# PSUM banks chosen by the scheduler, a reordered first load and warm-up matmuls in an eight-core decoder kernel

## Chip, cores and metric

The kernel runs on all 8 cores of one Trainium2 chip. The metric is the device time of the slowest core, in microseconds (us). The program has a second, slower state: in some executions the cores of one die get a lower clock, and the time is some per cent longer (in one slow run of experiment 9, cores 4 to 7 had a mean granted clock of 0.807 to 0.810 and the time was 1508.9 us, where the fast runs took 1339.9 and 1341.6 us). The granted clock is the share of TensorE's full clock that the chip granted, as the profile records it.

## The reference, cut to what matters

Two layers of a hybrid decoder. Each layer normalises its input, projects it into q, k, v, gates and a rank-16 "alpha_low", runs gated linear attention and a causal pooling mixer, and merges the two branches.

```python
xn = rmsnorm(h, norm_g)
q, k, v, ga, u, gb, alow, mg = jnp.split(xn @ w_in, IN_OFFSETS, axis=-1)
la = jax.nn.log_sigmoid(alow @ w_alpha + b_alpha) / GATE_TAU     # alow has 16 columns
...                                                              # linear attention with forget gate la
y_pool = pool_mix(u, 0, 0, pool_w, pool_scale)                   # trailing means over 2, 4, 8, 16
ya = (rms(o) * gla_gain * silu(ga)) @ w_a
yb = (y_pool * silu(gb)) @ w_b
return h + (s_a * ya + s_b * yb) @ w_out, S_new, buf_new
```

Each core takes one prompt of 2048 tokens and 16 samples of 4 tokens. The prompt is worked on in 16 token tiles of 128, two to a pair: pairs p0 to p7. The sample tokens and the 16 meta tokens form one more block of 80 columns, called p8. Phase 1 of a layer goes through p0 to p7 and then p8; phase 2 merges the branches.

## The kernel before

The program is recorded as a list of operations and then list-scheduled: each engine takes, among its operations that are ready, the one that stands first in the program. The program gives out 8 PSUM banks. Before, this is done in program order while the list is recorded, least recently freed first; the scheduler moves operations afterwards, but cannot change a bank.

```python
class Banks:
    def pair(self):                       # two neighbouring banks, freed longest ago
        c = [s for s in range(0, 8, 2) if s in self.freed and s + 1 in self.freed]
        s = min(c, key=lambda s: (max(self.freed[s], self.freed[s + 1]), s))
        del self.freed[s], self.freed[s + 1]
        return (s, s + 1)
    # ... one(), free()

def decay(l, p):
    n = ntok(p)                           # 256, or 80 for p8
    xn = xn_of(p)
    b1 = banks.one()
    for kc in range(8):                   # "alow": 16 weight columns
        mm(bank(b1)[0:16, 0:n], V1[:, kc * 16:kc * 16 + 16], xn[:, kc, 0:n], kc == 0, kc == 7)
    cp("act", alow[0:16, 0:n], bank(b1)[0:16, 0:n])      # one buffer "alow" for all pairs
    banks.free(b1)
    b2 = banks.pair()
    for h in range(4):                    # "alpha": 17 rows, fp32
        mm(bank(b2)[:, h * n:(h + 1) * n], walpha[0:17, h * 128:(h + 1) * 128], alow[0:17, 0:n], True, True)
    # ... exp, ln, scan, exp on ScalarE and VectorE

def v_proj(p, i):
    b_ = banks.pair()
    # ... 16 matmuls of 128x512, then one copy on ScalarE
    banks.free(b_)

def phase1(l):
    front(l, 0); front(l, 1)
    if l == 0:
        pace(len(queue), False)           # all weight loads
    decay(l, 0); decay(l, 1)
    # ... v of four tiles, then q, k of two pairs
    for p in range(NPAIR):
        if p >= 2:
            decay(l, p); v_proj(p, 0); v_proj(p, 1); q_proj(p); k_proj(p)
        # ... k_tok, gate_a, scores, attend, pool_u, attend
        gate_b(l, p)
        # ... normalise, gate_o, front(l, p + 2)
        pool_y(l, p)                      # needs the window sums of GpSimd
        # ... gate_o
    decay(l, NPAIR)                       # the block p8
    # ... the rest of p8
```

Of the kernel before, what the change touches and what calls it, by code (L numbers as in the profile page):

```python
# [49 lines left out]

class Sched:
# [4 lines left out]
    def __init__(self):  # L56
        self.ops = []
        self.last_w = {}
        self.readers = {}
        self.cache = {}  # L60

    def grains(self, x):
        if isinstance(x, (str, tuple)):
            return (x,)
        t = x.tensor.name
        esz = 4 if x.dtype == F32 else 2
        dims = [(int(s), int(n)) for s, n in x.ap]
        key = (t, esz, int(x.offset), tuple(dims))
        g = self.cache.get(key)
        if g is None:  # L70
            row = dims[0][0]
            lo = int(x.offset) % row
            hi = lo + sum(s * (n - 1) for s, n in dims[1:]) + 1
            if t == "psum":
                g = tuple(("B", b) for b in range(lo * esz // 2048, (hi * esz - 1) // 2048 + 1))
            else:
                g = tuple(range(lo * esz // GR, (hi * esz - 1) // GR + 1))
            self.cache[key] = g
        return g

    def add(self, eng, fn, r=(), w=(), dma=False, after=(), cost=300.0, lat=100.0, attach=False):
        i = len(self.ops)
        deps = {}
        rg = [g for x in r for g in self.grains(x)]
        wg = [g for x in w for g in self.grains(x)]
        excl = set(g for g in rg if isinstance(g, tuple) and g[0] == "B")
        for g in rg:
            d = self.last_w.get(g)
            if d is not None:
                deps[d] = "RAW"  # L90
        for g in excl:
            for e, d in self.readers.get(g, ()):
                if e != eng and d not in deps:
                    deps[d] = "WAR"
        for g in wg:
            d = self.last_w.get(g)
            if d is not None and d not in deps:
                deps[d] = "WAW"
            for _, d in self.readers.get(g, ()):
                if d not in deps:  # L100
                    deps[d] = "WAR"
        for d in after:
            if d is not None:
                deps[d] = "RAW"
        for g in rg:
            self.readers.setdefault(g, []).append((eng, i))
        for g in wg:
            self.last_w[g] = i
            self.readers[g] = []
        deps.pop(i, None)  # L110
        self.ops.append(dict(eng=eng, fn=fn, deps=deps, dma=dma, token=None, cost=float(cost), lat=float(lat),
                             attach=attach))
        return i
# [7 lines left out]
    def list_schedule(self):  # L121
        ops = self.ops
# [14 lines left out]
        for i in range(n):  # L137
            if npred[i] == 0:
                heapq.heappush(pend[ops[i]["eng"]], (0.0, i))
        order = []  # L140
        start_t = {}
        while len(order) < n:
            best = None
            for e in engs:
                T = free_t[e]
                while pend[e] and pend[e][0][0] <= T:
                    heapq.heappush(avail[e], heapq.heappop(pend[e])[1])
                if avail[e]:
                    st_, idx = T, avail[e][0]
                elif pend[e]:  # L150
                    st_, idx = pend[e][0]
                else:
                    continue
                if best is None or (st_, idx) < (best[0], best[1]):
                    best = (st_, idx, e)
            st_, idx, e = best
            if avail[e] and avail[e][0] == idx:
                heapq.heappop(avail[e])
            else:
                heapq.heappop(pend[e])  # L160
# [6 lines left out]
            else:  # L167
                free_t[e] = st_ + op["cost"]
                done_t[idx] = st_ + op["cost"] + op["lat"]
            order.append(idx)  # L170
# [156 lines left out]
class Banks:  # L327


    def __init__(self):  # L330
        self.freed = {b: b - 8 for b in range(8)}
        self.clock = 0

    def pair(self):
        c = [s for s in range(0, 8, 2) if s in self.freed and s + 1 in self.freed]
        assert c, "no pair of banks"
        s = min(c, key=lambda s: (max(self.freed[s], self.freed[s + 1]), s))
        del self.freed[s], self.freed[s + 1]
        return (s, s + 1)

    def one(self):
        lone = [b for b in self.freed if (b ^ 1) not in self.freed]
        c = lone or list(self.freed)
        assert c, "no bank"
        b = min(c, key=lambda b: (self.freed[b], b))
        del self.freed[b]
        return (b,)

    def free(self, bs):
        for b in bs:  # L350
            assert b not in self.freed
            self.clock += 1
            self.freed[b] = self.clock


def build_nc():
# [34 lines left out]
    with contextlib.ExitStack() as st:  # L391
# [3 lines left out]
        banks = Banks()  # L395
# [78 lines left out]
        vtok.append(bf(v2_off + 8192, 1024))  # L474

# [25 lines left out]
        def mm(out, lhsT, rhs, start, stop, sgc=False):  # L501
# [3 lines left out]
            return S.add("pe", lambda e: e.matmul(out, lhsT=lhsT, rhs=rhs, start=start, stop=stop,  # L505
# [3 lines left out]
        def tr(out, in_, ident):  # L509
            c = 58.0 if in_.dtype != F32 else 220.0  # L510
            return S.add("pe", lambda e: e.transpose(out, in_, ident), r=[in_, ident], w=[out], cost=c, lat=250.0,  # L511
                         attach=True)

        def act(out, in_, func, bias=None, scale=None, accum_out=None):
# [17 lines left out]
            return S.add("act", lambda e: e.activation(out=out, in_=in_, func=func, **kw), r=r, w=w, cost=c)  # L532
# [8 lines left out]
        def tt(eng, out, in0, in1, op):  # L541
# [3 lines left out]
            return S.add(eng, lambda e: e.tensor_tensor(out=out, in0=in0, in1=in1, op=op), r=[in0, in1], w=[out], cost=c)  # L545

        def ts(eng, out, in0, s1, s2=None, op0=ALU.mult, op1=None):
# [4 lines left out]
            return S.add(eng, lambda e: e.tensor_scalar(out=out, in0=in0, **kw), r=r, w=[out],  # L552
                         cost=ecost(eng, fsz(out), 0.55, [out] + r))

        def stt(out, in0, scalar, in1, op0, op1):
            r = [in0, in1] + ([] if isinstance(scalar, float) else [scalar])
            return S.add("dve", lambda e: e.scalar_tensor_tensor(out=out, in0=in0, scalar=scalar, in1=in1, op0=op0,  # L557
# [3 lines left out]
        def cp(eng, out, in_):  # L561
            if eng == "act":
                return act(out, in_, AF.Copy)
            return S.add(eng, lambda e: e.tensor_copy(out=out, in_=in_), r=[in_], w=[out],  # L564
# [15 lines left out]
        def bank(bs):  # L580
            return psum[:, bs[0] * 512:bs[0] * 512 + 512 * len(bs)]

        def bbank(bs):
            return psum[:, bs[0] * 512:bs[0] * 512 + 512].bitcast(BF16)
# [5 lines left out]
        cft = f32(base, NCF)  # L590
        dma(cft, cf_d[:, :])
        dma(cols, cols_d[:, :])
        for t in range(2):
            dma(hb[t], hin[128 * t:128 * (t + 1), :])
# [15 lines left out]
        W1V = [(0, O_V)] + [(O_V + 2048 * i, O_V + 2048 * (i + 1)) for i in range(8)]  # L610
# [41 lines left out]
        def norm_t(l, h, n, k, dst):  # L652
# [3 lines left out]
            b_ = banks.one()  # L656
# [5 lines left out]
            banks.free(b_)  # L662

        def front(l, p):

            if l == 0:
                for i, t in enumerate(tiles_of(p)):
                    r0, n = rows(t)
                    h = hb[t % 2][0:n, :]
                    if t >= 2:  # L670
                        dma(h, hin[r0:r0 + n, :], eng="pool" if t < 4 else "sp")
# [17 lines left out]
        def decay(l, p):  # L689
# [3 lines left out]
            b1 = banks.one()  # L693
# [3 lines left out]
            banks.free(b1)  # L697
            b2 = banks.pair()
# [4 lines left out]
            banks.free(b2)  # L703
# [25 lines left out]
        def q_proj(p):  # L729
# [3 lines left out]
            b_ = banks.pair()  # L733
# [3 lines left out]
            banks.free(b_)  # L737

        def k_proj(p):
# [3 lines left out]
            b_ = banks.pair()  # L743
# [3 lines left out]
            banks.free(b_)  # L747
# [4 lines left out]
        def v_proj(p, i):  # L752
# [4 lines left out]
            b_ = banks.pair()  # L757
            for b in range(2):
                for kc in range(8):
                    mm(bank(b_)[0:n, b * 512:(b + 1) * 512], xn[:, kc, i * 128:i * 128 + n],  # L760
                       WV[:, kc * 1024 + b * 512:kc * 1024 + (b + 1) * 512], kc == 0, kc == 7)
            cp("act", v_[0:n, :], bank(b_)[0:n, :])
            banks.free(b_)

        def k_tok(p, k_):

            n = ntok(p)
            b_ = banks.one()
# [17 lines left out]
            banks.free(b_)  # L786

        def scores(p, i, q_, k_):
            N = ntok(p)
            n = 128 if p < NPAIR else NM  # L790
            b_ = banks.one()
# [6 lines left out]
            banks.free(b_)  # L798
# [9 lines left out]
        def attend(p, i, q_, v_):  # L808

            t = tiles_of(p)[i]  # L810
            bo = banks.pair()
# [6 lines left out]
            bp = banks.pair()  # L818
# [9 lines left out]
            banks.free(bp)  # L828
            return bo

        def normalise(bo, n, dst, k):
# [12 lines left out]
            banks.free(bo)  # L844

        def gate_o(src, n, egv, dst):
            b_ = banks.one()
# [4 lines left out]
            banks.free(b_)  # L852

        def gate_a(l, p, r):
# [4 lines left out]
            b_ = banks.pair()  # L859
# [4 lines left out]
            banks.free(b_)  # L864
# [14 lines left out]
        def pool_u(l, p):  # L879
            n = ntok(p)  # L880
            xn = xn_of(p)
            b_ = banks.pair()
# [7 lines left out]
            if p < NPAIR:  # L890
                cp("act", ue[:, :, 15:271], u3)
                banks.free(b_)
# [13 lines left out]
            banks.free(b_)  # L906
# [10 lines left out]
        def pool_state(l):  # L917
# [3 lines left out]
            for rt in range(2):  # L921
                sp_ = xb[rt].bitcast(F32)[0:120, :]
                dma(sp_, spool[l].rearrange("s p c -> (s p) c")[rt * 120:(rt + 1) * 120, :])
                b_ = banks.one()
# [4 lines left out]
                banks.free(b_)  # L929

        def pool_out(l):
# [5 lines left out]
            b_ = banks.one()  # L937
# [4 lines left out]
            banks.free(b_)  # L942
            for k in range(TS):
                dma(nsp_s[l, :, 11 + k, :], tmpB[k * NSS:(k + 1) * NSS, 0:512])
            b_ = banks.one()
# [3 lines left out]
            banks.free(b_)  # L949
            dma(nsp_p[l], tmpB[0:15, 512:1024])  # L950

        def gate_b(l, p):
            n = ntok(p)
            xn = xn_of(p)
            b_ = banks.pair()
# [5 lines left out]
            banks.free(b_)  # L961

        def pool_y(l, p):
            n = ntok(p)
            b_ = banks.pair()
# [8 lines left out]
            banks.free(b_)  # L974
# [3 lines left out]
        def phase1(l):  # L978
            memset("dve", alow[0:17, :], 1.0)
            dma(walpha[0:17, :], walpha_d[l])  # L980
            front(l, 0)
            front(l, 1)
            if l == 0:
                pace(len(queue), False)
            decay(l, 0)
            decay(l, 1)
# [4 lines left out]
            for f_ in (q_proj, k_proj):  # L991
                for p in range(2):
                    f_(p)
                    if l > 0:
                        pace()
# [52 lines left out]
            bp = banks.pair()  # L1048
# [7 lines left out]
            banks.free(bp)  # L1056
# [17 lines left out]
        def sample_write(l, s, hp):  # L1074
            b_ = banks.one()
# [7 lines left out]
            banks.free(b_)  # L1083
# [3 lines left out]
        def sample_o(l, bT):  # L1087
            cp("act", oT_sb, bank(bT))
            banks.free(bT)
            bo = banks.pair()  # L1090
# [20 lines left out]
        def merge(l, j, c):  # L1111
# [7 lines left out]
            b_ = banks.pair()  # L1119
# [14 lines left out]
            banks.free(b_)  # L1134
# [9 lines left out]
        def out_tile(l, j, i):  # L1144
# [8 lines left out]
            b_ = banks.pair()  # L1153
# [5 lines left out]
            banks.free(b_)  # L1159
# [14 lines left out]
        def phase2(l):  # L1174
# [4 lines left out]
            bT = banks.one()  # L1179
# [102 lines left out]
```

## Time and profile before

| | before |
|---|---|
| median of 3 runs | 1356.64 us (1355.9 to 1439.92; the last is a slow run) |
| profiled run, slowest core | core 7, 1357.5 us, mean granted clock 0.960 |
| TensorE busy | 1226.7 us, 90% |
| TensorE busy in the first 68 us | 18.85 us |
| period of a pair, layer 0 (p3 to p6) | 44.1 to 44.7 us |
| period of a pair, layer 1 (p2 to p7) | 38.5 us |

A period is the time from one pair's last gate_b matmul to the next pair's. It is found by matching the recorded matmuls, in order, with the steps of the program; all marks below are taken so.

First, lines of the profile page of the kernel before: the busy time of each engine, and the granted clock of TensorE in 40 slices of the span, in tenths.

```profile
span 1357.5 us, 28419 instructions; the slowest of 8 cores (1347.9 to 1357.5 us)
...
PE 1226.7 (90%) x10600; PEld 945.8 (70%) x10600; DVE 626.6 (46%) x942; ACT 529.3 (39%) x1020; POOL 501.9 (37%) x850
...
PEclk9689889888999999989999999999999989999999
```

TensorE is what is nearly always busy. The clock row has nearly all its dips to 8 or less in the first ten slices (the start and layer 0's phase 1). In layer 1's phase 1 (slices 24 to 31) it stays at 9, which stands for 90% or more.

Next, the start of the same kernel in three stretches: window, its length, then for each engine busy us and instructions, then granted clock, DMA share (how busy the 16 DMA engines of the core were), GB/s.

```profile
core 7: us, PE busy (x) PEld busy (x) DVE busy (x) ACT busy (x) POOL busy (x), PEclk, DMA share, GB/s
0.00:68.00 68.00, 18.85 (x73) 9.58 (x73) 12.96 (x24) 12.29 (x17) 15.55 (x37) 0.82 0.98 177
68.00:80.00 12.00, 11.05 (x29) 5.18 (x30) 0.89 (x1) 3.14 (x4) 0.00 (x0) 0.50 0.73 187
80.00:118.00 38.00, 37.94 (x326) 30.78 (x324) 14.06 (x14) 13.62 (x25) 10.08 (x20) 0.99 0.05 15
```

While the weights load (DMA share 0.98), TensorE works 18.85 of 68 us. At 68 to 80 us it works off a backlog at a clock of 0.50.

The third view is the same for one pair boundary of layer 1, between p4 and p5.

```profile
core 7: us, PE busy (x) PEld busy (x) DVE busy (x) ACT busy (x) POOL busy (x), PEclk, DMA share, GB/s
918.00:921.00 3.00, 2.88 (x31) 2.43 (x28) 1.25 (x4) 1.00 (x4) 3.00 (x3) 1.00 0.00 0
921.00:924.00 3.00, 1.86 (x8) 0.71 (x9) 3.00 (x5) 1.40 (x5) 3.00 (x5) 1.00 0.62 175
924.00:927.00 3.00, 2.83 (x19) 1.41 (x18) 3.00 (x7) 0.67 (x3) 2.83 (x7) 1.00 0.33 31
927.00:930.00 3.00, 3.00 (x21) 2.12 (x20) 1.80 (x3) 0.46 (x2) 0.92 (x3) 1.00 0.90 207
```

TensorE waits a little over a microsecond at 921 to 924, then works on; the clock stays at 1.00. The groups of matmuls in that boundary, by shape, show why there is work. In "17*128 17x256", the first part is rows by columns of the array that the stationary operand fills, the second the moving operand; then come the number, the busy time and the mean ns of one.

```profile
L505 PE MATMUL psum<-arena 128*128 128x512 bf16 x32 | 7.8, 380 | 0.2 <-DVE arena L545 0.2
L505 PE MATMUL psum<-arena 17*128 17x256 f32 x8 | 2.0, 387 | 0.0
L505 PE MATMUL psum<-arena 128*16 128x256 bf16 x8 | 1.2, 274 | 0.2 <-DVE arena L557 0.2
```

The 32 matmuls of 128x512 are v projections of p5, placed by the scheduler around the decay matmuls (16 columns, or 17 rows) while GpSimd finishes the window sums of p4. The waits of TensorE over the whole pair (engine and line waited for, total us, times, longest) are small:

```profile
PE psum L505 <- POOL arena L552: 0.8, 1, 0.8
PE psum L505 <- DVE arena L557: 0.4, 2, 0.3
PE psum L505 <- DVE arena L545: 0.2, 1, 0.2
```

### The profile page before, as it was taken

What the parts mean: (1) busy time and instruction counts of PE and PEld (TensorE: products, weight loads), DVE (VectorE), ACT (ScalarE), POOL (GpSimd) and SP (SyncE); (2) the same over time, 40 slices, a digit from 0 to 9 for tenths busy, and PEclk for the clock granted to TensorE, in tenths of its full rate; (3) what the DMA queues carried; (4) which work ended last, traced back from release to release, by engine and by line L of the source; (5) the groups of instructions that cost most, each with busy time, mean ns of one, the idle gap of its engine ahead of it and who ended that gap; (6) DMA issues with size and microseconds to landing.
All of it is one profiled execution on the core that took longest, in us unless ns stands there. A gap on an engine that the chain in (4) does not pass through costs nothing.

```text
span 1357.5 us, 28419 instructions; the slowest of 8 cores (1347.9 to 1357.5 us)
## 1 busy us (share of the span) xinstructions
PE 1226.7 (90%) x10600; PEld 945.8 (70%) x10600; DVE 626.6 (46%) x942; ACT 529.3 (39%) x1020; POOL 501.9 (37%) x850
## 2 busy tenths in 40 slices
PE   3299889988998899989999989999998979999997
PEld 1067567666777688868775867777777858888875
DVE  2126564555546144444434375455556334444433
ACT  1124445444454233323335345544455223333332
POOL 3005453245437222332222364334456413323222
PEclk9689889888999999989999999999999989999999
DMA  9931221432126865889423510222231955665511
GB/s 169 186 83 55 86 58 41 98 76 47 38 49 155 182 204 186 220 216 244 169 89 104 97 68 27 51 67 67 67 67 29 207 160 182 183 206 179 179 68 63
DMA packets 47078, 160.29 MB, mean 118 GB/s; under 512 B 5772, under 2 KB 5900, under 8 KB 46908
## 3 DMA queue, kind: packets, MB, share of 16 engines
q1 hardware_dynamic: 35996, 121.44, 27.3%
q0 software_dynamic: 10944, 37.03, 17.8%
q8 instruction: 83, 1.36, 0.4%
q14 instruction: 55, 0.45, 0.1%
HBM read 139.98 MB, written 55.18 MB: 144 GB/s over the span
## 4 chain that ended last, share of the span: by engine, by line
PE 70%; DMA 10%; POOL 7%; DVE 5%; issue 4%; ACT 2%; SPq 0%; POOLq 0%; DVEq 0%; ACTq 0%
PE psum L505 68%; DVE arena L557 4%; POOL arena L545 4%; DMA arena<-hin 4%; POOL arena L552 3%; PE psum L511 2%; DMA arena<-w 2%; DMA arena<-sgla 2%; ACT arena L532 2%; DMA nsg_s<-arena 1%; DMA nsp_s<-arena 1%; DVE arena L545 0%; DVE arena L706 0%; SPq L577 0%; ACT L532 0%
## 5 line engine op out<-in xcount | busy, mean ns | idle before, releaser
L505 PE MATMUL psum<-arena 128*128 128x256 bf16 (+4 forms) x9888 | 1189.2, 280 | 71.6 <-DVE arena L557 27.0
L505 PEld LDWEIGHTS psum<-arena 128*128 128x128 bf16 (+2 forms) x9888 | 898.9, 100 | 337.7 <-issue 43.0
L557 DVE SCALAR_TENSOR_TENSOR arena<-arena,psum 128x256 f32<-128x256 f32 (+4 forms) x454 | 261.4, 607 | 305.3 <-PE psum L505 197.9
L545 POOL TENSOR_TENSOR arena<-arena 128x256 bf16<-128x256 f32 (+13 forms) x321 | 280.6, 878 | 246.8 <-DVE arena L557 227.0
L532 ACT ACTIVATE arena<-psum 128x256 bf16<-128x256 f32 (+9 forms) x308 | 200.4, 660 | 349.9 <-PE psum L505 240.5
L552 POOL TENSOR_SCALAR arena<-arena 128x256 bf16<-128x256 f32 (+5 forms) x389 | 167.5, 438 | 420.0 <-DVE arena L557 192.1
L532 ACT ACTIVATE arena<-psum,arena 128x256 f32<-128x256 f32 (+2 forms) x356 | 145.0, 455 | 232.9 <-PE psum L505 194.2
L532 ACT ACTIVATE arena<-arena 128x1024 bf16<-128x1024 f32 (+2 forms) x137 | 138.6, 1027 | 213.9 <-DVE arena L557 136.0
L545 DVE TENSOR_TENSOR arena<-psum,arena 128x1024 bf16<-128x1024 bf16 (+4 forms) x120 | 123.5, 1040 | 120.7 <-PE psum L505 81.2
L557 DVE SCALAR_TENSOR_TENSOR arena<-psum,arena 128x256 bf16<-128x256 f32 (+4 forms) x124 | 91.8, 763 | 123.5 <-PE psum L505 114.8
L511 PE MATMUL psum<-arena 128*128 128x128 bf16 (+4 forms) x712 | 64.5, 234 | 50.2 <-DVE arena L552 44.0
L511 PEld LDWEIGHTS psum<-arena 128*128 128x128 bf16 (+4 forms) x712 | 51.0, 106 | 64.5 <-DVE arena L552 45.7
L706 DVE TENSOR_TENSOR_SCAN arena<-arena 128x1024 f32<-128x1024 bf16 (+1 forms) x18 | 40.6, 2256 | 81.3 <-ACT arena L532 81.3
L577 POOL DMA_DIRECT2D arena<-w x74 | 43.9, 598 | 88.8 <-DMA OT<-arena 56.7
L557 DVE SCALAR_TENSOR_TENSOR arena<-arena 128x256 bf16<-128x256 f32 (+4 forms) x97 | 64.6, 674 | 24.8 <-POOL arena L545 24.5
L552 DVE TENSOR_SCALAR arena<-arena 128x1024 bf16<-128x1024 f32 (+4 forms) x45 | 29.0, 660 | 50.6 <-POOL arena L545 44.8
L532 ACT ACT_TABLE_LOAD x32 | 41.1, 1283 | 25.2 <-PE psum L505 14.4
L564 POOL COPY arena<-arena 128x4 f32<-128x4 f32 (+4 forms) x56 | 12.3, 219 | 92.2 <-ACT arena L532 89.4
L552 DVE TENSOR_SCALAR arena<-psum,arena 128x256 bf16<-128x256 f32 (+1 forms) x68 | 29.7, 477 | 15.9 <-ACT arena L532 11.0
L532 ACT ACTIVATION_READ_ACCUMULATOR arena<-psum 128x1 f32 (+1 forms) x136 | 26.8, 197 | 0.0
L532 ACT ACTIVATION_READ_ACCUMULATOR arena<-arena 128x1 f32 (+1 forms) x51 | 9.6, 188 | 0.0
L564 DVE COPY arena<-psum 128x1024 f32<-128x1024 f32 x2 | 2.5, 1225 | 2.6 <-PE psum L505 2.6
(9 smaller groups left out, 5.6 us busy)
## 6 DMA issues: line engine op xcount, KB each, us to landing
arena<-w POOLq DMA_DIRECT2D x38, 512.0 KB, 14.9
arena<-sgla SPq DMA_DIRECT2D x32, 512.0 KB, 7.3
nsg_s<-arena SPq DMA_DIRECT2D x32, 512.0 KB, 4.3
arena<-hin SPq DMA_DIRECT2D x30, 512.0 KB, 5.0
arena<-w POOLq DMA_DIRECT2D x32, 448.0 KB, 5.7
arena<-XN SPq DMA_DIRECT2D x22, 512.0 KB, 4.9
H<-arena SPq DMA_DIRECT2D x16, 512.0 KB, 3.1
arena<-H SPq DMA_DIRECT2D x16, 512.0 KB, 4.8
```

What stands on the lines that cost most here:

```text
L505: return S.add("pe", lambda e: e.matmul(out, lhsT=lhsT, rhs=rhs, start=start, stop=stop, skip_group_check=sgc), r=[lhsT, rhs], w=[out], co ...
L511: return S.add("pe", lambda e: e.transpose(out, in_, ident), r=[in_, ident], w=[out], cost=c, lat=250.0, attach=True)
L532: return S.add("act", lambda e: e.activation(out=out, in_=in_, func=func, **kw), r=r, w=w, cost=c)
L545: return S.add(eng, lambda e: e.tensor_tensor(out=out, in0=in0, in1=in1, op=op), r=[in0, in1], w=[out], cost=c)
L552: return S.add(eng, lambda e: e.tensor_scalar(out=out, in0=in0, **kw), r=r, w=[out], cost=ecost(eng, fsz(out), 0.55, [out] + r))
L557: return S.add("dve", lambda e: e.scalar_tensor_tensor(out=out, in0=in0, scalar=scalar, in1=in1, op0=op0, op1=op1), r=r, w=[out], cost=eco ...
L564: return S.add(eng, lambda e: e.tensor_copy(out=out, in_=in_), r=[in_], w=[out], cost=ecost(eng, fsz(out), 0.55, (out, in_)))
L577: return S.add(eng, lambda e: e.dma_start(out=out, in_=in_, **kw), r=list(r) + sb_r, w=list(w) + sb_w, dma=True, after=after, cost=nb / (3 ...
L706: S.add("dve", lambda e: e.tensor_tensor_scan(out=B, data0=rm[:, 0:4 * n], data1=A, initial=0.0, op0=ALU.mult, op1=ALU.add), r=[rm[:, 0:4 ...
```

## The change

The intent is fourfold. The scheduler chooses PSUM banks when it places the first operation of a tile (here, one use of one or two PSUM banks), so that no order is frozen by program order. One rule comes with it, called the reserve rule below: the last free pair of banks is kept for the oldest tile. The first load queue is interleaved, so that q, k and v of the first two pairs can run while the gate weights still load; for this tiles 2 and 3 get buffers of their own and v's weights are laid out in two halves. The start of phase 1 is put in that order as well. And 14 matmuls, called the warm-up, stand at the start.

```diff
+def place(t):                                  # inside the list scheduler
+    whole = [q for q in range(0, 8, 2) if max(freed[q], freed[q + 1]) < inf]
+    spare = t.tid == oldest                     # oldest tile that has no bank yet
+    if t.n_banks == 2:
+        if not whole or (len(whole) < 2 and not spare):
+            return inf, None                    # the last free pair is kept for the oldest
+        ...
+    lone = [b for b in range(8) if freed[b] < inf and freed[b ^ 1] == inf]
+    if not lone and len(whole) < 2 and not spare:
+        return inf, None
...
-            b1 = banks.one()
+            b1 = S.tile(1)                      # likewise everywhere; banks.free() goes
...
+        wt = S.tile(1)
+        for _ in range(14):
+            mm(bank(wt), rm_b[:, 0:128], rm_b[:, 128:640], True, True)
...
-        W1V = [(0, O_V)] + [(O_V + 2048 * i, O_V + 2048 * (i + 1)) for i in range(8)]
+        W1V = [(0, O_V)] + [(O_V + 2048 * i, O_V + 2048 * (i + 1)) for i in (4, 5, 6, 7, 0, 1, 2, 3)]
...
-                    h = hb[t % 2][0:n, :]
+                    h = (hb2 if t in (2, 3) else hb)[t % 2][0:n, :]
...
-            front(l, 0)
-            front(l, 1)
-            if l == 0:
-                pace(len(queue), False)
-            decay(l, 0)
-            decay(l, 1)
+            for p in range(2):
+                if p == 0 and l == 0:
+                    pace(5, False)
+                front(l, p)
+                decay(l, p)
+                for f_ in (q_proj, k_proj):
+                    f_(p)
+                    if l > 0:
+                        pace()
+                if p == 1 and l == 0:
+                    pace(len(queue), False)
```

## The prediction

> **What bounds it now.** TensorE: 1226.7 of 1357.5 us busy (page, busy table). Its 131 us of idle time lies in three places.
> 1. Start. TensorE is busy only 18.9 us of the first 68 (windows), while the DMA share is 0.94 to 1.03. Token tiles 2 and 3 stand behind ten or more weight pieces in the GpSimd queue and land about 30 us after issue (chain of waits); TensorE stops in its order on them until 68.9 us. The loads end at 76 us; the backlog (four v, q, k, gates) then runs at clock 0.50 until about 80. The first pair's gate_b ends at 117 us.
> 2. Pair boundaries, layer 0: period 44.6 us, 5 us idle each (2.98 + 1.89), after which the clock falls to half. Layer 1: 38.5 us, 1.5 to 3 us idle, clock 1.00.
> 3. Phase changes (about 450 and 1090 us), DMA share 1.0: some 8 us each.
> Phase 2 has TensorE 97 to 100% busy: nothing to win.
>
> **Start.** The queue becomes alpha, q, k, tiles 2 and 3, v, gates; tiles 2 and 3 get their own buffers. Bytes are unchanged, so loads still end near 73 to 76 us (17 pieces of about 3.4 us of all engines, plus hin and XN). But q, k and v of pairs 0 and 1 now run under the load instead of after it (183 matmuls took 31 us after 68.9). gate_b of pair 0 needs the last pieces, so it should end near 79 us instead of 117; idle in pair 0's tail gives a little back. Estimate: -36 us.
>
> **Warm-up matmuls.** They run in time that is idle anyway. [...] worth under 1 us.
>
> **Bank choice, layer 0 pairs 2 to 5.** GpSimd and VectorE orders are the same; on TensorE decay and six v matmuls move before the last gate transposes, but behind the same VectorE wait. About 0.
>
> **Bank choice, layer 1.** The placing rule keeps a pair of banks for the oldest tile, so v of the next pair can no longer fill the wait for the GpSimd window chain. Before, 15 v matmuls (3.2 us) and 3 q ran before the gate transposes; now all 32 v follow them. That chain (GpSimd, 910.3 to 926.5 us without a break) sets the period: it shortens by 0.5 us, while 3.4 us of matmuls move behind it. Estimated period 41 to 43 us, the upper end if the 5 us near-idle stretch halves the clock, as it does in layer 0. Five pairs: +14 to +24; pair 6 of layer 0 and pair 0 of layer 1: +4. Phase changes stay DMA-bound: -3.
>
> **Sum.** 1357 - 36 + 23 - 3 = 1341 us. Range 1320 to 1360. Chances: faster 0.27, same 0.71, slower 0.02.
>
> **Right if:** bulk of pair 2's projections starts near 118 us instead of 154; loads still end near 75; layer-0 periods stay 44 to 45; layer-1 periods grow to 41 to 43 with TensorE idle before pool_y and the gate transposes and a dip of the clock there; phase 2 lasts as long as before.
>
> **Wrong if:** layer-1 periods stay at 38.5 (then about 1320), because the earlier normalisation shortens the chain more than I count; the start gains less because tiles 2 and 3 still land late or the clock stays at half under the load (then 1350 or more); or layer 0's boundary gaps close (4 x 5 us, then below 1325).

In the warm-up paragraph the ground for "under 1 us", a rule on the clock and a comparison with it, is cut, since no trace here shows it; the "under 1 us" stands as the author's estimate. No term of the sum is cut: it still comes to 1357 - 36 + 23 - 3 = 1341 us. Two of its figures, as the trace of the kernel before has them: the queue that brings the weights took 79.0% of the first 76 us of all engines for 9.60 MB, which is 3.3 us per 512 KB; and at a boundary of layer 0 the clock was 0.51 at 238 to 240 us and 0.50 from 240 to 244, where the waits of TensorE were 2.98 us (to 238.7) and 1.89 us (to 241.6).

## More of the kernel before

Lines L532, L545, L552, L557 of this kernel are the helpers for activations, tensor_tensor, tensor_scalar and scalar_tensor_tensor; L505 is the matmul and L511 the transpose. In the changed kernel they are L620, L633, L640, L645, L593 and L599.

## The result, and the profile after

| | before | after |
|---|---|---|
| median of 3 runs | 1356.64 us | 1395.32 us (1395.24 to 1395.6) |
| ratio of fast runs | | 1.0288, 95% interval 1.0259 to 1.0318 |
| profiled run, slowest core | core 7, 1357.5 us | core 2, 1393.4 us |
| mean granted clock, all cores | 0.960 to 0.964 | 0.931 to 0.939 |
| TensorE busy | 1226.7 us | 1273.7 us |
| period of a pair, layer 1 (p2 to p7) | 38.5 us | 45.3 to 47.2 us on core 2 |

Ratios here are the mean time of one kernel's fast runs over the mean of the other's fast runs of the same rounds, so they are not quite the ratio of the medians.

The kernel became slower by 2.9%. Busy time grew by 47 us though only 14 matmuls were added: the same matmuls took longer. The page of the changed kernel, same lines as before:

```profile
span 1393.4 us, 28474 instructions; the slowest of 8 cores (1382.0 to 1393.4 us)
...
PE 1273.7 (91%) x10614; PEld 967.0 (69%) x10614; DVE 628.2 (45%) x942; ACT 527.0 (38%) x1020; POOL 498.5 (36%) x850
...
PEclk7899999988998999999999898999889989999999
```

The start did what it was meant to do:

```profile
core 2: us, PE busy (x) PEld busy (x) DVE busy (x) ACT busy (x) POOL busy (x), PEclk, DMA share, GB/s
0.00:68.00 68.00, 50.92 (x268) 30.33 (x269) 20.84 (x30) 19.62 (x26) 19.67 (x41) 0.77 0.98 192
68.00:80.00 12.00, 12.00 (x118) 10.58 (x115) 4.86 (x5) 7.06 (x13) 2.93 (x7) 1.00 0.89 149
80.00:118.00 38.00, 32.65 (x292) 27.02 (x289) 25.39 (x42) 19.02 (x46) 27.87 (x47) 0.91 0.17 63
```

TensorE now works 50.92 of the first 68 us, and at a clock of 1.00 just after. The boundary of the same pair of layer 1 (p4 to p5) looks quite different:

```profile
core 2: us, PE busy (x) PEld busy (x) DVE busy (x) ACT busy (x) POOL busy (x), PEclk, DMA share, GB/s
930.00:933.00 3.00, 0.78 (x9) 0.36 (x6) 2.75 (x4) 1.02 (x1) 2.80 (x6) 1.00 0.10 25
933.00:936.00 3.00, 1.51 (x7) 0.64 (x8) 2.73 (x8) 0.84 (x2) 2.74 (x5) 0.82 1.02 263
936.00:939.00 3.00, 3.00 (x13) 2.06 (x12) 1.54 (x2) 0.00 (x0) 0.00 (x0) 0.50 0.45 131
939.00:942.00 3.00, 3.00 (x8) 1.43 (x7) 0.00 (x0) 0.88 (x1) 0.09 (x1) 0.50 0.43 175
942.00:945.00 3.00, 3.00 (x8) 1.06 (x7) 0.33 (x1) 2.48 (x3) 0.55 (x1) 0.50 0.62 90
945.00:948.00 3.00, 3.00 (x15) 1.31 (x14) 1.96 (x1) 1.02 (x1) 0.00 (x0) 0.97 0.32 63
```

At 930 to 936 TensorE is busy for only 2.3 of 6 us. Then it is busy all the time, but at a clock of 0.50, for some 10 us, from about 935 to 945 us. A fall to half over 10 us costs about 5 us (an estimate: half of the time at half clock; in this run 48 matmuls of 128x512 kept TensorE busy for 10.5 us at a clock of 1.00, 734 to 744 us, and 10 of them for 4.4 us at 0.50, 939 to 945 us, so 0.22 and 0.44 us each). The shapes in this stretch:

```profile
L593 PE MATMUL psum<-arena 128*128 128x512 bf16 x24 | 7.4, 484 | 0.0
L593 PE MATMUL psum<-arena 17*128 17x256 f32 x8 | 3.8, 649 | 0.0
L593 PE MATMUL psum<-arena 128*16 128x256 bf16 x4 | 1.2, 402 | 1.1 <-DMA arena<-XN 1.1
```

The v matmuls took 484 ns each in place of 380, the alpha matmuls 649 ns in place of 387. The waits of the whole pair on TensorE:

```profile
PE psum L593 <- DVE arena L645: 3.6, 3, 2.3
PE psum L593 <- DMA arena<-XN: 1.1, 1, 1.1
PE psum L593 <- ACT arena L620: 0.3, 1, 0.3
```

It is now 5.0 us in all, 3.6 of it on VectorE and 1.1 on a load, where it was 1.4 us.

The ledger below compares the two profiled runs. A column gives how far the changed kernel is ahead (minus) or behind (plus) when the step ends.

| mark | before, us | after, us | difference | change since the last row |
|---|---|---|---|---|
| layer 0, gate_b of p0 | 117.5 | 85.8 | -31.7 | -31.7 |
| layer 0, gate_b of p5 | 323.1 | 287.9 | -35.1 | -3.4 |
| layer 0, gate_b of p7 | 405.7 | 381.4 | -24.3 | +10.8 |
| end of layer 0 | 740.3 | 715.8 | -24.4 | -0.1 |
| layer 1, gate_b of p1 | 805.0 | 791.7 | -13.3 | +11.1 |
| layer 1, gate_b of p7 | 1035.8 | 1069.8 | +34.0 | +47.3 |
| last matmul of the program | 1348.5 | 1384.6 | +36.1 | +2.1 |

The start and the pairs p2 to p5 gained 35 us. All of it and more was lost in phase 1, chiefly in six pairs of layer 1.

There the loss can be split from the two traces. In the six pairs TensorE was busy for 222.0 of 230.8 us before and for 252.0 of 278.1 us after, with the same matmuls. So 30.0 us of the 47.3 us are the same matmuls taking longer (mean granted clock 1.00 before, 0.89 after), and 17.3 us are added waits.

One thing in the trace gave the first theory. The line below is from the changed kernel at 720.6 to 721.0 us, the very start of layer 1; the moving operand of 80 columns belongs to p8, and 16 weight columns mean its alow product.

```profile
L593 PE MATMUL psum<-arena 128*16 128x80 bf16 x8 | 0.5, 201 | 0.0
```

The matching alpha product of p8 (17 rows, 80 columns) runs 352 us later:

```profile
L593 PE MATMUL psum<-arena 17*128 17x80 f32 x8 | 1.3, 286 | 0.1
```

p8's input is ready early, so the new placer gives its alow product a bank at once. But its result goes to the one buffer alow, which the program gives to p8 only after p7. So a bank is held through the whole of layer 1's phase 1. With one bank gone, 3 whole pairs are left, and one of them is reserved for the oldest tile. In the kernel before, p8's alow product ran at 1040.5 us and its alpha product at 1045.2.

### The profile page after: what moved, and what is told of

Its sections match the earlier page's. It is cut to its first block, busy times and chain, and to the rows that moved or that the text cites. A ratio compares the mean times of both kernels' runs of the same rounds, so it can differ in the third digit from the quotient of the medians.

```text
span 1393.4 us, 28474 instructions; the slowest of 8 cores (1382.0 to 1393.4 us)
## 1 busy us (share of the span) xinstructions
PE 1273.7 (91%) x10614; PEld 967.0 (69%) x10614; DVE 628.2 (45%) x942; ACT 527.0 (38%) x1020; POOL 498.5 (36%) x850
## 4 chain that ended last, share of the span: by engine, by line
PE 76%; DMA 8%; POOL 5%; DVE 4%; issue 4%; ACT 2%; SPq 0%; DVEq 0%; POOLq 0%; ACTq 0%
PE psum L593 74%; POOL arena L633 3%; DMA nsp_s<-arena 3%; DVE arena L645 3%; PE psum L599 3%; DMA arena<-w 2%; ACT arena L620 2%; POOL arena L640 2%; DMA arena<-sgla 1%; DVE arena L633 1%; DMA arena<-XN 1%; DVE arena L640 0%; DMA arena<-hin 0%; SPq L665 0%; DVEq L369 0%
## 5 line engine op out<-in xcount | busy, mean ns | idle before, releaser
L593 PE MATMUL psum<-arena 128*128 128x256 bf16 (+5 forms) x9902 | 1232.7, 285 | 87.3 <-DVE arena L645 36.9
L593 PEld LDWEIGHTS psum<-arena 128*128 128x128 bf16 (+2 forms) x9902 | 918.7, 102 | 373.7 <-issue 75.7
L633 POOL TENSOR_TENSOR arena<-arena 128x256 bf16<-128x256 f32 (+14 forms) x321 | 275.4, 863 | 271.2 <-DVE arena L645 246.7
L620 ACT ACTIVATE arena<-psum 128x256 bf16<-128x256 f32 (+10 forms) x308 | 199.5, 659 | 362.5 <-PE psum L593 259.9
L599 PE MATMUL psum<-arena 128*128 128x128 bf16 (+3 forms) x712 | 67.7, 239 | 23.6 <-DVE arena L640 13.4
L599 PEld LDWEIGHTS psum<-arena 128*128 128x128 bf16 (+3 forms) x712 | 51.9, 108 | 43.5 <-DVE arena L640 15.4
L645 DVE SCALAR_TENSOR_TENSOR arena<-arena 128x256 bf16<-128x256 f32 (+4 forms) x97 | 66.5, 699 | 26.2 <-POOL arena L633 24.4
L640 DVE TENSOR_SCALAR arena<-arena 128x1024 bf16<-128x1024 f32 (+4 forms) x45 | 33.2, 755 | 37.1 <-POOL arena L633 30.4
L640 DVE TENSOR_SCALAR arena<-psum,arena 128x256 bf16<-128x256 f32 (+1 forms) x68 | 29.6, 477 | 38.4 <-POOL arena L633 27.2
```

The lines of the kernel that those rows point to most:

```text
L593: return S.add("pe", lambda e: e.matmul(ready(out), lhsT=lhsT, rhs=rhs, start=start, stop=stop, skip_group_check=sgc), r=[lhsT, rhs], w=[o ...
L599: return S.add("pe", lambda e: e.transpose(ready(out), in_, ident), r=[in_, ident], w=[out], cost=c, lat=250.0, attach=True)
L620: return S.add("act", lambda e: e.activation(out=out, in_=ready(in_), func=func, **kw), r=r, w=w, cost=c)
L633: return S.add(eng, lambda e: e.tensor_tensor(out=out, in0=ready(in0), in1=in1, op=op), r=[in0, in1], w=[out], cost=c)
L640: return S.add(eng, lambda e: e.tensor_scalar(out=out, in0=ready(in0), **kw), r=r, w=[out], cost=ecost(eng, fsz(out), 0.55, [out] + r))
L645: return S.add("dve", lambda e: e.scalar_tensor_tensor(out=out, in0=ready(in0), scalar=scalar, in1=ready(in1), op0=op0, op1=op1), r=r, w=[ ...
```

## The experiments

Thirteen kernels ran, all with correct results. "Static banks" are those of the kernel before, given out while the program is recorded. The theories: A, a bank held early by p8 costs the time; B, the reserve rule alone, as predicted, costs it; C, the new load and program order costs it; D, the granted clock halves on sparse matmuls and turns a small wait into a large one. Times are medians of all runs of a kernel; where slow runs were among them, the fast ones are given.

### 1. Delay p8 alone

```diff
+        alpha_mm = []
         def decay(l, p):
...
-                mm(bank(b1)[0:16, 0:n], V1[...], xn[:, kc, 0:n], kc == 0, kc == 7)
+                mm(bank(b1)[0:16, 0:n], V1[...], xn[:, kc, 0:n], kc == 0, kc == 7,
+                   after=alpha_mm if p == NPAIR else ())       # p8 waits for p7's alpha
```

> The changed kernel with one dependence added: the 8 alpha_low matmuls of the last block (decay of p8) may start only after the alpha matmuls of pair 7. Theory A (a bank held too early: in the changed kernel these 8 matmuls stand at the very start of layer 1, and their bank stays taken until pair 7 is through, so no pair of banks is left for v): layer-1 pair period back from 46.5 to 38 to 40 us, no clock dips in layer 1, total 1325 to 1345 us. Theory B (the rule that keeps a pair of banks for the oldest tile is enough by itself, as predicted): period stays over 44 us, total 1380 or more. Theory C (the new load and program order at the start of layer 1 does it): no change, 1390 or more.

The edit delays p8's alow in both layers. Fast runs 1355.3 and 1354.4 us (two more were slow, so that the median is 1426.77); ratio to before 0.9973 (0.9951 to 0.9994). Periods of layer 1 fell from 45 to 47 us to 37.9, 39.6 or 41.2 us, with the reserve rule still in place. So A holds for layer 1 and B falls as the only cause; but the expected total (1325 to 1345 us, no dips of the clock) was missed. The three values differ by steps of 1.6 and 1.7 us; what sets the steps was not shown. One boundary of this kernel, same columns as before:

```profile
907.00:910.00 3.00, 2.25 (x20) 1.30 (x18) 2.46 (x4) 2.29 (x6) 3.00 (x4) 1.00 0.62 156
910.00:913.00 3.00, 2.89 (x9) 1.96 (x9) 2.74 (x6) 0.00 (x0) 2.84 (x6) 0.69 0.41 50
913.00:916.00 3.00, 3.00 (x9) 1.06 (x8) 1.23 (x4) 1.86 (x2) 1.69 (x4) 0.50 0.66 130
916.00:919.00 3.00, 3.00 (x11) 1.12 (x10) 1.81 (x3) 2.23 (x4) 0.00 (x0) 0.68 0.23 87
```

The clock falls to 0.69 and 0.50 although TensorE is busy for 5.14 of the 6 us from 907 to 913. In the kernel before, it was busy for 4.69 of 6 us (921 to 927) and kept 1.00. This is where theory D came from. What differs is which matmuls ran: here the sparse decay products come in a block, there v products lie between them.

### 2. Take the reserve rule away

```diff
-                if not whole or (len(whole) < 2 and not spare):
+                if not whole:
                     return inf, None
...
-            if not lone and len(whole) < 2 and not spare:
-                return inf, None
```

> The changed kernel without the rule that keeps a pair of banks for the oldest tile; the early bank of p8's decay stays (it stands at the second pair of layer 1 in this order). Theory A: period stays over 43 us, total 1375 to 1400. Theory B: v fills the gaps again, period 38 to 40, total 1325 to 1345. Theory C: 1390 or more.

Fast runs 1378.3 and 1377.0 us, ratio 1.0141 (1.0119 to 1.0163). Periods of layer 1 are 42.0 to 45.1 us for p3 to p6, 49.6 for p2 and 39.7 for p7. p8's alow product still ran early (at 789 us) and held its bank. So without the rule some 2 us per pair come back on average (263.8 us for the six pairs p2 to p7, against 278.1), but not the rest: the hold costs without the rule too.

### 3. Only the new start, on static banks

The load order, program order, buffers and warm-up of the changed kernel, on the bank choice of the kernel before.

> Start of the change (load queue, tile buffers, program order of the first two pairs in both layers, warm-up) on the old bank allocation. Theories A and B: first pair ends about 30 us earlier, layer 1 stays at 38.5 us a pair, total 1320 to 1335. Theory C: layer 1 slow here too, total 1360 or more.

1335.34 us, ratio 0.9833 (0.9815 to 0.9851). The gain of the start (27.8 us at p0) is kept to the end (26.7 us), and periods of layer 1 are 38.4 to 38.5. So C falls.

### 4. Only the new bank choice

The reverse: the changed kernel's placer with the start of the kernel before and no warm-up.

> Bank choice by the scheduler on the old start, no warm-up. In this order the last block's decay of layer 1 stands late, after pair 7, by itself; in layer 0 it stands in pair 6. Theory A: layer 1 at 38 to 40 us a pair, only pairs 6 and 7 of layer 0 lose some 10 us: total 1350 to 1372. Theory B: layer 1 over 44 us a pair, total 1400 or more. Theory C: as before, 1350 to 1365.

1359.61 us, ratio 1.0015 (0.9988 to 1.0042). The bank choice alone already gains 24.7 us at p0 and 31.9 at p5, so the gains of the two parts do not add. Here p8's alow product of layer 1 happened to be placed late (1036.9 us), and periods of layer 1 are 37.8 to 41.2. In layer 0 it was placed early (344.0 us, its alpha product at 393.3), and pairs 6 and 7 lost 16.6 us. But p8's alow is not needed for that loss. In experiment 1 it ran late in layer 0 as well (381.4 us), and pairs 6 and 7 still lost 10.3 us. Another tile of p8 was early in layer 0 in all three kernels: the transposes of its pool state, spread over 296.0 to 325.6 us in the changed kernel, 296.1 to 325.7 in experiment 1 and 299.2 to 329.0 here, that is through pair 6, with one bank held. In the kernel before they start at 407.5 us, after p7.

### 5. Limit the look-ahead

```diff
         def place(t):
+            if t.tid > oldest + 12:
+                return inf, None
```

> The changed kernel with one more rule: a tile may be given a bank only if it is at most 12 tiles younger than the oldest tile without one. The reserve rule stays. Both early holds (the decay of block 8 and the front of later pairs, in layer 0 and in layer 1) become impossible. If unlimited look-ahead is the whole cost: pair periods of layer 1 are 37.9 to 41.2 us as in the run that only delayed block 8; the losses of pairs 5 to 7 of layer 0 (11 us between pair 5 and the first out tile of layer 0 in that run, from -35.0 to -24.7) mostly vanish, so the first out tile of layer 0 stands at -25 or better against the kernel before instead of -16.5; time 1335 to 1350 us. If the reserve rule or the load order costs: layer 0 pair 6 keeps a period of 49 us and the time is 1352 or more.

1355.61 us, ratio 0.9992 (0.9971 to 1.0013): slower than expected. p8's alow and its pool state ran late in both layers, and layer 1 behaved as in experiment 1. On the core whose trace is used (core 0), pairs 6 and 7 of layer 0 lost 3.8 us in place of 10.8; on the other cores that could be matched, 1.0 to 7.3 us. But the first out tile of layer 0 was at -17.4 and not at -25, since pairs 2 and 3 took 46.6 and 46.5 us there (42.7 and 43.0 in the changed kernel). The look-ahead was not the whole of it.

### 6. Useless matmuls in the waits

```diff
+            for _ in range(16 if l == 1 and p < NPAIR else 0):
+                mm(bank(b_)[:, 0:512], rm_b[:, 0:128], rm_b[:, 128:640], True, True, after=last_gb)
             for g in range(4):               # the pooled projection, overwrites them
```

> The changed kernel with 16 useless 128x512 matmuls (3.4 us of TensorE at full clock) per pair of layer 1, in the bank pair of the pooled projection, after the pair's last gate_b matmul, so just where TensorE waits. Bank choice and reserve rule stay. If the long periods of layer 1 (44.9 to 47.1 us) hold the halved clock [...]after a stretch of sparse matmuls: the granted clock is 1.00 at the pair boundary and the period shrinks to 42 to 44 us although there is more work; the total falls by 10 to 25 us against the changed kernel (1370 to 1385). If the clock is not part of it, the period stays or grows by up to 3.4 us: 1395 to 1420 us.

Fast runs 1362.4 to 1365.7 us: 31 us faster than the changed kernel, with some 3.5 us of useless work added to every pair of layer 1 (an estimate: 16 matmuls at the 0.22 us of one at a clock of 1.00). The periods are 41.2 to 41.4 us for most pairs. The clock at the boundary after p4:

```profile
917.00:920.00 3.00, 3.00 (x22) 1.74 (x21) 2.27 (x3) 1.03 (x1) 2.80 (x5) 1.00 0.49 89
920.00:923.00 3.00, 3.00 (x18) 1.58 (x15) 2.33 (x7) 0.84 (x2) 3.00 (x6) 1.00 0.96 233
923.00:926.00 3.00, 3.00 (x18) 1.52 (x18) 2.43 (x5) 1.04 (x2) 0.23 (x1) 1.00 0.29 100
```

It stays at 1.00 where the changed kernel had 0.50 for 10 us. p8 still held its bank. This points to a split: with the clock up, the hold and the wait chain cost about 3 us per pair, which is what the prediction had counted. The run changes more than the clock, though (the filler also delays the pooled projection, and p6's decay moved). The split of the traces above, which needs no filler, gives nearly the same (17.3 us of waits in six pairs, 2.9 a pair), and experiment 12 checks it again.

### 7. Hold one bank, on static banks

```diff
             dma(walpha[0:17, :], walpha_d[l])
+            held = banks.one() if l == 1 else ()
...
+            banks.free(held)
             decay(l, NPAIR)
```

> The kernel before with static bank choice, and one PSUM bank withheld from the start of layer 1 until the decay of block 8; nothing else is changed. If the bank held so long is in itself the cost, periods of layer 1 grow from 38.5 to 41 us or more (six of them: 1372 or more). If a hold costs only together with the reserve rule of the new placer (which then never gives v its banks early), the periods stay at 38.5 to 39.5 and the time at 1357 to 1364 us.

Fast runs 1407.3 to 1409.4 us, ratio 1.0381 (1.0360 to 1.0402): the slowest of all. Periods of layer 1 went from 38.5 to 43.5 to 44.9 us. There is no new placer and no reserve rule here, so a bank held through the layer is costly by itself. The waits of TensorE in one pair, p5 after p4:

```profile
PE psum L505 <- DVE arena L557: 4.7, 4, 1.6
```

That is 4.7 us on VectorE in place of 0.4 in the kernel before. So this run puts a price on one bank withheld: 34 us over six pairs (265.2 us against 230.8).

### 8. Useless matmuls in layer 0

The kernel of experiment 3, with 13 useless matmuls before each pooled projection of layer 0 and 8 behind it.

> The static-bank kernel with the new start (1335 us in its run) plus useless matmuls in layer 0 alone: 13 before each pooled projection and 8 behind it, in the 2.98 us and 1.89 us in which TensorE waits for VectorE at each pair boundary. If the halved clock after each boundary (0.50 for about 6 us, of which some 3 us are busy) is a cost, periods of layer 0 (44.5 us) fall by 1 to 2 us for five pairs: 1325 to 1332 us. If VectorE alone sets the period of layer 0, or the added matmuls delay it, 1335 to 1345 us.

1348.87 us, 13 us slower than experiment 3: a miss. Periods of layer 0 rose from about 44.5 us to 45 to 47, and p7's from 38.6 to 41.8. The boundary after p3 on core 0 shows that the clock did stay up there (1.00), but also that the filler missed its place:

```profile
217.00:220.00 3.00, 0.36 (x3) 0.10 (x1) 3.00 (x5) 2.66 (x8) 3.00 (x5) 1.00 0.00 0
220.00:223.00 3.00, 2.59 (x13) 1.19 (x14) 2.90 (x4) 0.00 (x0) 2.78 (x7) 1.00 0.61 87
223.00:226.00 3.00, 3.00 (x23) 1.78 (x22) 2.90 (x8) 0.84 (x2) 1.94 (x5) 1.00 0.79 241
```

The 2.98 us wait (3.0 us on VectorE in experiment 3, core 0) was for VectorE to empty the very bank pair into which the filler writes. The filler could only start after the wait (at 220.4 us), and so delayed the rest. Filler that needs the very banks waited for could not help here, and this run does not tell what the half clock costs in layer 0.

### 9. Wide decay matmuls

The kernel of experiment 1, in which only the decay products of p2 to p7 of layer 1 are made to fill the array. The number of matmuls, their moving columns, and the order of all TensorE work stay.

```diff
+            w, k = (128, 128) if l == 1 and 2 <= p < NPAIR else (16, 17)
-                mm(bank(b1)[0:16, 0:n], V1[:, kc * 16:kc * 16 + 16], ...)
+                mm(bank(b1)[0:w, 0:n], V1[:, kc * 16:kc * 16 + w], ...)   # rows 16.. are not read
-                mm(..., walpha[0:17, h * 128:(h + 1) * 128], alow[0:17, 0:n], ...)
+                mm(..., walpha[0:k, h * 128:(h + 1) * 128], alow[0:k, 0:n], ...)   # rows 17.. are zero
```

> The kernel of the first experiment (block 8 delayed), with the decay matmuls of pairs 2 to 7 of layer 1 widened: the low-rank product uses 128 weight columns instead of 16 (the further rows of its result are not read) and the alpha product 128 rows instead of 17 (the further ones zero). Count, order, output and the streamed columns stay; results stay correct. If matmuls that fill little of the array count as idle for the clock: the granted clock stays at 1.00 at all pair boundaries of layer 1 and all periods are 37.9 (first experiment: 37.9 to 41.2, mean about 39.7), the time falls by 5 to 12 us against the first experiment: 1341 to 1348. If only true waiting counts: the same scatter of periods from 37.9 to 41.2, 1352 to 1356 us.

Fast runs 1339.9 and 1341.6 us against 1355.3 and 1354.4 of experiment 1 (two more runs were slow; against the kernel before in the same rounds the ratio is 1340.8 / 1356.0 = 0.989). All periods of layer 1 are 37.4 to 37.5 us, on every core whose matmuls could be matched. The boundary after p4:

```profile
900.00:903.00 3.00, 2.16 (x20) 1.30 (x17) 2.40 (x3) 2.35 (x6) 3.00 (x4) 1.00 0.50 152
903.00:906.00 3.00, 2.89 (x15) 2.04 (x15) 3.00 (x7) 0.60 (x1) 2.84 (x6) 1.00 0.33 49
906.00:909.00 3.00, 3.00 (x16) 1.37 (x14) 1.39 (x5) 2.91 (x4) 1.63 (x4) 1.00 0.92 215
```

The stretch from 900 to 906 us is as empty as in experiment 1 (5.05 of 6 us busy against 5.14), yet the clock stays at 1.00. And the alpha products, now 128 rows:

```profile
L593 PE MATMUL psum<-arena 128*128 128x256 f32 x8 | 2.1, 392 | 0.1
```

They take 392 ns; 17 rows had taken 387 ns in the kernel before, at a clock of 1.00. So filling the array cost 5 ns per alpha matmul here, and the clock stayed at 1.00. This is the strongest evidence for D: busy time is nearly equal, the order and the banks of all TensorE work are equal, and only the part of the array in use differs, in the matmuls and in the loads of their weights (the two were not told apart).

### 10. Wide decay matmuls on static banks

The kernel of experiment 3, widened for p2 to p7 of both layers.

> The static-bank kernel with the new start (1335 us in its run), with the decay matmuls of pairs 2 to 7 widened in the same way in both layers. Its layer 1 has no fall of the clock, so nothing can be gained there; in layer 0 the clock falls in a true wait of 3 us followed by another of 1.9 us, before the decay. If sparse matmuls only prolong a fall that a true wait started: 1 us or less per pair of layer 0, 1329 to 1335 us. If widening itself costs (longer weight loads): 1336 to 1345.

Fast runs 1327.4 to 1330.5 us (one of four was slow), ratio 0.9799 (0.9781 to 0.9817) against 0.9833 (0.9815 to 0.9851) of experiment 3; the intervals just overlap. The total is as expected, its place is not: layer 1's periods went from 38.5 to 38.0, where nothing had been expected, and those of layer 0 hardly moved. This fits a fall in layer 0 that starts in true waits: in experiment 3 (core 2) the clock is 0.77, 0.50 and 0.59 in the three stretches of 3 us from 211 to 220 us, in which TensorE is busy for 0.88, 0.71 and 3.00 us, and 1.00 after that. As to the weight loads: in the kernel before (700 to 1100 us) a bf16 load took 92 ns on average with 16 columns and 99 ns with 128. Why layer 1 gains 0.5 us is not settled.

### 11. No warm-up

The changed kernel without its 14 warm-up matmuls.

> The changed kernel without its 14 warm-up matmuls. If they are worth something, the first gate_b ends later than 85.8 us and the time rises above 1395 by the same. If they run in time that is idle anyway [...]: within 2 us of the changed kernel at every mark.

Fast runs 1392.4 to 1397.5 us, ratio 1.0286 (1.0263 to 1.0308) against 1.0288 with them. The first gate_b ended at 86.1 us, with warm-up at 85.8. Later marks differ by up to 4.0 us (gate_b of p6 in layer 0), more than the 2 us expected, but on another core and chip, and by 1.7 us at the last matmul. In the total they are worth nothing measurable.

### 12. The changed kernel itself, with wide decay matmuls

The edit of experiment 9 in the changed kernel: same banks, same order, p8 still holding its bank.

> The changed kernel with nothing changed but the width of the decay matmuls of pairs 2 to 7 in layer 1 (as in the ninth experiment). Banks, order on every engine, number and streamed columns of all matmuls stay; block 8 still holds its bank. If the halved clock is what the prediction undersized: periods of layer 1 fall from 44.9-47.1 to 41-42.5 us, the same on all cores, and the time to 1362 to 1374. If the true waits alone (2.3 us before the pooled projection) halve the clock, or the bank held is the whole cost: periods of 44 or more, 1385 to 1395.

Fast runs 1374.0 and 1376.1 us, ratio 1.0116 (1.0094 to 1.0137). Periods of layer 1 are 41.0 to 44.7 us for p2 to p6 and 39.5 to 39.7 for p7, so the expectation of 41 to 42.5 was only half met. The boundary shows why:

```profile
921.00:924.00 3.00, 0.51 (x5) 0.10 (x1) 2.90 (x4) 0.91 (x1) 2.80 (x5) 1.00 0.69 169
924.00:927.00 3.00, 2.14 (x12) 1.37 (x13) 2.88 (x8) 0.84 (x2) 2.25 (x5) 0.55 0.78 161
927.00:930.00 3.00, 3.00 (x12) 2.46 (x10) 1.22 (x1) 0.00 (x0) 0.00 (x0) 0.50 0.33 130
930.00:933.00 3.00, 3.00 (x13) 1.46 (x12) 0.00 (x0) 1.78 (x2) 0.63 (x1) 0.82 0.32 132
```

From 921 to 924 us TensorE was busy for 0.51 us. After this true wait the clock is 0.55 and then 0.50, although no matmul of 16 columns or 17 rows ran from 921 to 936 us; but the half clock now lasts about 7 us and not 10 (both worked out from the windows' mean clocks). So here both work together: the fall starts at the wait, and lasts 3 us longer where the decay matmuls behind it are sparse.

### 13. Look-ahead limit and wide decay matmuls

Experiments 5 and 9 together, widened in both layers.

> The changed kernel with the look-ahead limit of the fifth experiment and wide decay matmuls for pairs 2 to 7 in both layers. Layer 1 periods 37.5 throughout (five of six cores-pairs saw 39.6 to 41.2 without it). If the look-ahead was the cause of the layer 0 loss and the clock of what remained there: first out tile of layer 0 at -25 us or better against the kernel before, time 1318 to 1330. If the reserve rule costs in layer 0: first out tile at -15 to -18 as before and 1332 to 1345.

1328.04 us (1327.5 to 1330.1), ratio 0.9774 (0.9756 to 0.9791), the best of all and 2.3% faster than before. Layer 1 runs at 37.5 us per pair. In layer 0 the lead is -36.5 us at p5 and -35.9 at p7: the loss of pairs 6 and 7 is gone, which the look-ahead limit alone had not achieved.

The six pairs p2 to p7 of layer 1, from gate_b of p1 to gate_b of p7, in one table (one core each):

| kernel | bank held | mean granted clock | six pairs, us | per pair |
|---|---|---|---|---|
| before | no | 1.00 | 230.8 | 38.5 |
| after | yes | 0.89 | 278.1 | 46.3 |
| 12: after, wide | yes | 0.94 | 257.8 | 43.0 |
| 6: after, filler | yes | 0.99 | 249.1 | 41.5 |
| 2: after, no reserve rule | yes | 0.92 | 263.8 | 44.0 |
| 7: before, hold | yes | 0.95 | 265.2 | 44.2 |
| 1: p8 late | no | 0.94 | 242.0 | 40.3 |
| 9: p8 late, wide | no | 1.00 | 224.8 | 37.5 |
| 13: window, wide | no | 1.00 | 224.9 | 37.5 |

## Why the prediction was right or wrong

**The start: right in the main.** Predicted -36 us, with gate_b of p0 near 79 us; it ended at 85.8, and the gain was -31.7 at p0 and -29.4 at p1. That the lead at p5 is -35.1, so near the -36, is luck: pairs 2 to 5 added what the start lacked. A thing not foreseen: the bank choice alone brings most of it (experiment 4).

**Warm-up: right.** Predicted under 1 us; the first gate_b differs by 0.3 us and the ratio to before by 0.0002 (experiment 11). In the changed kernel's trace the 14 matmuls take 5.0 us (2.7 to 7.8 us), and at 12 to 30 us the clock is 0.50 all the same.

**Layer 0, pairs 2 to 5: a little off.** Predicted about 0; measured -5.7 us from p1 (-29.4) to p5 (-35.1), of which -3.3 came in pair 2.

**Phase 2 unchanged: right.** In layer 1 it lasts 220.4 us from the start of its third block to the end, in both. The phase changes brought -0.1 and +2.1 us in place of -3.

**Layer 1, the term that failed.** The prediction said: "Estimated period 41 to 43 us, the upper end if the 5 us near-idle stretch halves the clock", and "Five pairs: +14 to +24". Measured were 45 to 47 us, six pairs (p7 was left out of the sum) and +47.3 us. The direction was right, and that v would all follow the gate transposes was right. Two things were wrong in the step:

1. The size of the clock's part. The added waits are 17.3 us in six pairs, 2.9 us per pair, and with the clock kept up by filler the period is 41.5 us, inside the predicted range; so the chain of waits had been costed about right. The clock's fall adds about 30 us over six pairs (the growth of busy time; 278.1 - 249.1 = 29.0 by experiment 6), 5 us per pair, where the prediction allowed for at most 2. What it missed is that the clock stays low through the sparse decay products behind the wait (0.50 from about 935 to 945 us after p4). Filling the array in them, in the same order and banks, takes back 20.3 us (278.1 - 257.8).
2. The mechanism. It named the reserve rule. Without the held bank the rule is still there, and costs 1.9 us per pair at most (40.3 in experiment 1 against 38.5 before). Even that goes through the clock: with wide decay products, experiment 9 runs at 37.5 us with the rule, and the static banks of experiment 10 at 38.0 without it. The cause is that p8's decay takes a bank at 720 us and gives it back after p7, because nothing limits the look-ahead; the rule then makes it worse (experiment 2). One held bank is costly with static banks and no rule as well (experiment 7).

**Pair 6 of layer 0 and pair 0 of layer 1: too small.** Predicted +4; measured +10.8 for p6 and p7 of layer 0 and +11.1 up to p1 of layer 1. In layer 0 p8's alow comes early too, but only at 339.5 us, after the gate_b of p6 (337.0), so it can't be what made pair 6 long (49.1 us). What holds a bank through pair 6 is the pool state of p8 (296.0 to 325.6 us, experiment 4). With a look-ahead limit and wide decay products both run after p7, and the loss there is 0.6 us; a run that delays the pool state alone was not made, so this cause is likely but not shown. At the start of layer 1 the early alow of p8 is part of the loss: from the end of layer 0 to gate_b of p1 it is 64.7 us before, 75.9 after, and 71.0 in experiment 1; a bank withheld from static banks made it 79.6 (experiment 7). The rest, 6.8 us in experiment 13 (-36.1 to -29.3), static banks alone avoid (experiment 3); its cause stays open.

The sum then: -35.1 + 10.8 - 0.1 + 11.1 + 47.3 + 2.1 = +36.1 us, where -16 had been predicted. The error of 52 us consists of about 23 to 33 us in the six pairs of layer 1 that the prediction had in its sum as +14 to +24 for five, 18 us at the two seams, 5 us at the phase changes and 1 us at the start and pairs 2 to 5 of layer 0 together.

## What to carry to other kernels

A scheduler that gives out a scarce buffer when an operation becomes ready needs a limit on how far ahead it may look, or a check that the buffer will be released soon; an operation that is ready early but is consumed late can hold it for a quarter of the run (352 of 1393 us here). When a wait on TensorE grows by a few microseconds, look at the granted clock behind it before costing it: what followed at a lowered clock cost more than the waits here (30.0 us against 17.3 in six pairs). Where low-rank matmuls stand behind such a wait, put full-array work between them (the clock was 1.00 in the kernel before, with v products between) or fill the array with unused columns and zero rows (1.00 in experiment 9), which cost 5 ns per alpha matmul here (392 against 387).
